# Block products for two gates: seven-product units, weight sums by accumulating transfers

## The chip, the cores and the metric

One core of a Trainium2 chip runs the whole kernel. The metric is the time of one execution on the device in microseconds (us); lower is better. Work is spread over five engines with instruction streams of their own: TensorE (PE) multiplies matrices, VectorE (DVE), ScalarE (ACT) and GpSimd (POOL) work on elements, SyncE (SP) issues transfers. DMA queues move data between DRAM and the on-chip memory. An engine executes its stream in order, and an instruction waits at the head of its stream until what it needs has been signalled.

## The reference

One step of a hybrid diffusion transformer on 128 context tokens and 512 latent tokens, 640 in all, with D = 1024. What bears on the change:

```python
def retention_branch(rq, rk, rv, rg, pos, dec_f, dec_b, s0_f, s0_b):
    ...
    o = rms_scale(o_f + o_b[:, :, ::-1])
    o = o.transpose(0, 2, 1, 3).reshape(B, L, RET_V)
    return jax.nn.silu(rg.astype(jnp.float32)) * o, s_f, s_b

def token_mixer(h, w_in, ...):
    z = h @ w_in
    q, k, v, rq, rk, rv, rg, ga, gr = jnp.split(z, np.cumsum(IN_SPLITS)[:-1].tolist(), axis=-1)
    ...
    ya = attend_blocks(q, k_all, v_all)
    yr, s_f, s_b = retention_branch(rq, rk, rv, rg, ret_pos, dec_f, dec_b, s0_f, s0_b)
    y = jax.nn.sigmoid(ga) * (ya @ w_att_o) + jax.nn.sigmoid(gr) * (yr.astype(h.dtype) @ w_ret_o)
    return y @ w_out, (k, v, s_f, s_b)
```

`rg` (1024 columns of w_in) is the output gate inside the retention branch, `gr` (1024 columns) the gate of the whole branch. After the mixer come a normalisation and a gated feed-forward part with a depthwise convolution (FFN).

## The kernel before

The tokens are five tiles of 128. Each matrix product is made of three: every operand is split into a high part (rounded to fp32r by ACT) and a low part (the rest, by DVE), and high x high, high x low and low x high are summed in PSUM. Weights come into `raw` buffers by SP's queue (two buffers of up to 1 MB, `w_raw`), their parts into `wh` buffers. ACT can also make a low part with DVE left out: it writes the negated weights, and a transfer issued by POOL adds the weights to it while it writes (an accumulating DMA; L150, L1148).

The stages around the change, in the order in which PE does them:

- States and retention (`states`, `retention`, until 498 us), with the first half of rg's columns (`rg0`) between its steps. `conv_load` (L1005) loads the constants of the FFN's convolution by four DMAs of SP, at step 1 of the retention (three of L1008, one of L1009). The reloads of the retention's queries, `qd` (L955), are in the same queue behind them.
- The second half of rg's columns by `a_group` (L175): five tiles of 128 tokens, the weights' 512 columns moving, 8 blocks of the inner dimension, 3 products: 120 matmuls of 512 columns. `evac_rg` (L1035) makes silu out of tanh and multiplies it onto `rvv`, the retention's normalised output.
- gr's columns by `gr_col` and `b_col` (L191): eight blocks of 128 columns as stationary operand, two halves of 320 tokens moving, 8 x 3 matmuls each: 384 of 320 columns. ACT writes the tanh of each half to `thr` (L1105). Between the first of them PE transposes `rvv` to yr (`yr_blocks`, L1067; ten blocks, each with four transpositions into one PSUM bank, and a split into a high and a low part). `ret_sums` builds the sums of quarters of yr on DVE (L1085 to L1097).
- `ret_unit` (four, from 586 us): yr @ w_ret_o for two blocks of 128 columns each. A unit is a two by two block product done with seven products of half sized blocks in place of eight; each product is four blocks of the inner dimension x 3 = 12 matmuls of 320 columns. The weight blocks B00, B01, B10, B11 are summed on DVE (`wsum`, L1131), the activations' quarters beforehand (`ret_sums`).

The seven products are numbered 1 to 7. 1, 6, 7 and 4 share one PSUM bank and pile up in it: ACT copies the bank out after 1 (L1181), after 6 (negated, L1185), after 7 (L1189) and after 4 (L1193), each before the next product is added into the bank. 2 has a bank of its own, 5 and 3 share a third. From the m=5 sum on, the buffer of B00 serves 5 (B00 + B01), then 6 (with B11 added), then 4 (with B10 added). `ret_pump` (L1219) queues the weights' preparation some products ahead, and `seq` is the order of the products in which product 4 of a unit is held back until two products of the next unit have been issued. PE, DVE and ACT keep the order of the code in these last two stages (`manual_schedule`); a scheduler orders the others and what is ahead.

## Time and profile before

| | |
|---|---|
| median of three runs | 1137.73 us (1137.13 to 1139.15) |
| profiled execution, time | 1138.44 us |
| its span, first to last instruction | 1136.7 us |
| its granted clock of TensorE | 0.998 of full speed |
| busy: PE, DVE, ACT, POOL | 1109.3, 844.2, 594.5, 142.9 us |
| retention ends, second half of rg | 498.5 to 525.8 us |
| gr with the transposition of yr | 525.8 to about 586 us |

A row of the timeline has start, length, engine, line, operation, output<-inputs, shape, and in brackets how long the engine had been idle and what ended that. A matmul's length includes its way through the array, so the rate of a row of them is read from the distance of their starts. A wait row names what waited, what it waited for, the total, how often, and the longest. "Landing" of a DMA is the time from its issue to its end.

### The profile page before, as it was taken

What the parts mean: (1) busy time and instruction counts of PE and PEld (TensorE: products, weight loads), DVE (VectorE), ACT (ScalarE), POOL (GpSimd) and SP (SyncE); (2) the same over time, 40 slices, a digit from 0 to 9 for tenths busy, and PEclk for the clock granted to TensorE, in tenths of its full rate; (3) what the DMA queues carried; (4) which work ended last, traced back from release to release, by engine and by line L of the source; (5) the groups of instructions that cost most, each with busy time, mean ns of one, the idle gap of its engine ahead of it and who ended that gap; (6) DMA issues with size and microseconds to landing.
All of it is one profiled execution on the core that took longest, in us unless ns stands there. A gap on an engine that the chain in (4) does not pass through costs nothing.

```text
span 1136.7 us, 17580 instructions
## 1 busy us (share of the span) xinstructions
PE 1109.3 (98%) x6757; PEld 1009.6 (89%) x6757; DVE 844.2 (74%) x1456; ACT 594.5 (52%) x1120; POOL 142.9 (13%) x171
## 2 busy tenths in 40 slices
...
GB/s 307 246 152 74 39 37 38 2 37 215 323 146 174 243 115 110 78 38 38 74 72 163 302 132 212 130 112 121 143 139 158 157 80 167 130 128 155 136 130 93
DMA packets 139316, 151.99 MB, mean 134 GB/s; under 512 B 27976, under 2 KB 108952, under 8 KB 138976
## 3 DMA queue, kind: packets, MB, share of 16 engines
...
q10 hardware_dynamic: 272, 0.11, 0.0%
...
## 4 chain that ended last, share of the span: by engine, by line
PE 88%; DVE 5%; ACT 3%; issue 2%; DMA 1%; SPq 0%; ACTq 0%; DVEq 0%; POOL 0%
DMA weights.raw.247_7726<-in_w_down 1%; DVE x1.u1.1_6330 L1496 1%; DMA ret2.qd.12_4681<-ret.u5.5_3422 0%; DMA const.u2.2_72<-in_b_mod 0%; DVE x1.u1.1_6330 L1545 0%; DVE x1.u1.1_6330 L1303 0%; PE mm3.mm.75_6171 L1176 0%; DVE acts.u2.2_91 L432 0%; PE mm1.mm.11_294 L161 0%; PE mm7.mm.59_10668 L1619 0%; PE mm7.mm.17_8071 L1619 0%; PE mm7.mm.41_9543 L1619 0%; PE mm7.mm.59_10668 L1618 0%; PE mm7.mm.44_9776 L1618 0%; PE mm7.mm.38_9294 L1619 0%
## 5 line engine op out<-in xcount | busy, mean ns | idle before, releaser
L1148 POOL DMA_DIRECT2D weights.wh.164_5865<-weights.raw.156_5798 x1 | 1.3, 1327 | 146.9 <-DVE f1.s.15_5209 L1187 146.9
L816 POOL DMA_DIRECT2D spill.u2.2_2891<-f1.s.1_1160 x1 | 0.6, 580 | 129.7 <-DVE mod.u3.3_2846 L604 129.7
L1633 DVE TENSOR_TENSOR t7.u4.4_6818<-t7.u4.4_6818,const.u1.1_70 128x320 f32<-128x320 f32 x10 | 4.9, 494 | 11.4 <-ACT const.u1.1_70 L1632 11.4
L152 DVE TENSOR_TENSOR weights.wh.113_4453<-weights.raw.111_4450,weights.wh.112_4452 128x1024 fp32r<-128x1024 f32 x1 | 1.2, 1227 | 13.1 <-ACT weights.wh.112_4452 L147 13.1
L938 DVE SCALAR_TENSOR_TENSOR ret2.u1.1_4263<-ret2.u1.1_4263,const.u11.11_86 64x128 f32<-64x128 f32 x24 | 6.8, 338 | 2.9 <-ACT ret2.u1.1_4263 L931 2.8
L940 DVE SCALAR_TENSOR_TENSOR ret2.u1.1_4263<-ret2.u1.1_4263,const.u11.11_86 64x128 f32<-64x128 f32 x24 | 6.6, 382 | 2.8 <-ACT ret2.u1.1_4263 L933 2.8
L429 ACT CAST acts.u1.1_90<-f0.s.2_104 128x640 fp32r<-128x640 f32 x4 | 2.9, 728 | 9.5 <-DVE f0.s.2_104 L427 9.5
L553 ACT ACTIVATE f0.s.3_710<-f0.s.3_710,p1q.ny20.11_878 128x128 f32<-128x128 f32 x20 | 6.0, 388 | 2.5 <-DVE p1q.ny20.11_878 L220 2.5
L446 PE MATMUL aux1.aux.1_134<-const.u1.1_70,const.u2.2_72 80*128 80x80 f32 x1 | 0.4, 367 | 7.1 <-DMA const.u2.2_72<-in_b_mod 7.1
L429 ACT CAST acts.u1.1_90<-f0.s.1_103 128x640 fp32r<-128x640 f32 x4 | 2.9, 727 | 8.3 <-DVE f0.s.1_103 L427 8.3
L299 POOL DMA_DIRECT2D mod.acc.24_3630<-in_b_mod x2 | 1.7, 858 | 42.5 <-ACT ret.u5.5_3422 L874 42.5
L147 ACT CAST weights.wh.67_3284<-weights.raw.66_3282 128x1024 fp32r<-128x1024 f32 x1 | 1.1, 1052 | 11.3 <-PE mm3.mm.8_3125 L198 11.3
L147 ACT CAST weights.wh.77_3520<-weights.raw.76_3518 128x1024 fp32r<-128x1024 f32 x1 | 1.0, 1048 | 11.2 <-PE mm3.mm.16_3382 L198 11.2
L584 POOL TENSOR_TENSOR p1.u1.1_604<-p1.u3.3_608,p1q.u1.1_598 128x512 f32<-128x512 f32 x1 | 1.3, 1302 | 44.5 <-DMA p1.u4.4_610<-in_cache_k 44.5
L1150 DVE TENSOR_TENSOR weights.wh.152_5717<-weights.raw.151_5663,weights.wh.152_5717 128x512 fp32r<-128x512 f32 x1 | 0.7, 693 | 8.3 <-ACT weights.wh.152_5717 L1141 8.3
L147 ACT CAST weights.wh.132_5219<-weights.raw.131_5217 128x1024 fp32r<-128x1024 f32 x1 | 1.1, 1055 | 11.0 <-PE mm3.mm.49_5037 L160 11.0
L1507 DVE TENSOR_TENSOR x1.u1.1_6330<-x1.u1.1_6330,gate.u1.1_6316 128x512 f32<-128x512 f32 x10 | 6.7, 693 | 0.0
L553 ACT ACTIVATE p1.u4.4_610<-p1.u4.4_610,p1.ny10.15_660 128x128 f32<-128x128 f32 x10 | 3.0, 389 | 6.5 <-DVE p1.ny10.15_660 L220 6.5
L1540 POOL TENSOR_TENSOR x1.u1.1_6330<-x1.u1.1_6330,weights.raw.422_10889 128x512 f32<-128x512 f32 x3 | 4.9, 1632 | 12.2 <-ACT x1.tm.111_10902 L1513 9.4
L446 PEld LDWEIGHTS aux1.aux.1_134<-const.u1.1_70,const.u2.2_72 80*128 80x128 f32 x1 | 0.2, 182 | 7.0 <-issue 7.0
L152 DVE TENSOR_TENSOR weights.wh.83_3656<-weights.raw.81_3653,weights.wh.82_3655 128x1024 fp32r<-128x1024 f32 x1 | 1.2, 1226 | 6.9 <-ACT weights.wh.82_3655 L147 6.9
L553 ACT ACTIVATE f0.s.4_959<-f0.s.4_959,p1q.ny20.20_1127 128x128 f32<-128x128 f32 x20 | 6.2, 396 | 0.0
...
## 6 DMA issues: line engine op xcount, KB each, us to landing
...
p0.u7.7_128<-in_w_mod SPq DMA_DIRECT2D x2, 1024.0 KB, 12.3
...
out_y_sample<-x1.u1.1_6330 SPq DMA_DIRECT2D x8, 256.0 KB, 2.2
```

Source lines behind the costliest of these rows:

```text
L147: nc.scalar.copy(hi, rv)
L152: (lo_eng or V).tensor_sub(lo, rv, hi.bitcast(F32))
L299: nc.gpsimd.dma_start(accs[v][0:1, c, :], a["b_mod"][0:1, col:col + DM], accum_op=ALU.add)
L429: nc.scalar.copy(hT[0][:, k, :], xk)
L553: nc.scalar.activation(x[:, j], x[:, j], AF.Copy, scale=rstd[:, j:j + 1])
L584: nc.gpsimd.tensor_mul(ct, r2[:, :, 0, :], gqk[:, i:i + 1, :].to_broadcast([P, 4, P]))
L938: V.scalar_tensor_tensor(Ss[0:64, hh, st + 1, j], Ss[0:64, hh, st, j], cdsel[0:64, h:h + 1], Ss[0:64, hh, st + 1, j], op0=ALU.mult, op1=AL ...
L940: V.scalar_tensor_tensor(Ss[64:128, hh, 2 - st, j], Ss[64:128, hh, 3 - st, j], cdsel[64:128, h:h + 1], Ss[64:128, hh, 2 - st, j], op0=ALU. ...
L1496: V.tensor_add(x1[:, t, gs], x1[:, t, gs], down_mul(ps, t, c0))
L1507: V.tensor_mul(x1[:, t, gs], x1[:, t, gs], gb[:, t == 0, gs])
L1540: eng.tensor_mul(x, x, fg[:, c0:c0 + 512])
L1633: V.tensor_sub(his[1], his[1], u3[i])
```

## The change

rg's second half and all of gr are computed by six units like the `ret_unit`s: `in_unit` (L1152), two for rg's four blocks of columns and four for gr's eight, each with seven products of 12 matmuls of 320 columns, in the order 1, 5, 2, 6, 3, 7, 4. The common part of both kinds of unit is `seven`, the activations' sums are built by `h_sums` during states and retention, partly by accumulating transfers of 655 KB. In an `in_unit` DVE makes only B00 + B01; the other three sums come from w_in in DRAM by accumulating transfers of 256 KB (L1179 and L1180 after the low part of m=5, L1182 after that of m=6). The low parts of m=2, and in four of the six units of m=3, come by an accumulating transfer too (L1173).

rg's second half is now there in transposed form, in `thr`; silu is applied there (`rg_col`), and the transposed second half of yr is multiplied with it (`yr_block`). yr's ten blocks are transposed one at a time between products (`when`), and so are the pieces of yr's sums; `y_diff` has one of its three operations done by an accumulating transfer (655 KB). Product 4 of the first six units is held back for 2, 2, 4, 4, 4, 2 products.

In `retention`, `conv_load` is called for one row at a time, at steps 2, 4, 6 and 8. `rg0`'s low parts come by accumulating transfers ("dma"). Some buffers move: the constants' row buffer, one of the rope tables, a sixth `r2k` buffer less, the `f1` buffers closed before the states.

```diff
-    def conv_load(after):
-        nc.gpsimd.tensor_copy(cw[:, :, 0], after)
-        for i in range(3):
-            nc.sync.dma_start(cw[:, i, :], a["conv_w"][0, i].rearrange("(c p) -> p c", p=P))
-        nc.sync.dma_start(cw[:, 3, :], a["conv_b"][0].rearrange("(c p) -> p c", p=P))
+    def conv_load(i, after):
+        nc.gpsimd.tensor_copy(cw[:, i, :1], after)
+        src = a["conv_w"][0, i] if i < 3 else a["conv_b"][0]
+        nc.sync.dma_start(cw[:, i, :], src.rearrange("(c p) -> p c", p=P))
...
-            if i == 1:
-                conv_load(sa[0][2][:, :4])
+            if i in (2, 4, 6, 8):
+                conv_load(i // 2 - 1, sa[i - 1][2][:, :1])
...
-    rg0 = a_group(w_in[:, O_RG:O_RG + 512], hTk, mm, evac_rg(0))
+    rg0 = a_group(w_in[:, O_RG:O_RG + 512], hTk, mm, evac_rg(0), "dma")
...
-    run(a_group(w_in[:, O_RG + 512:O_RG + 1024], hTk, mm, evac_rg(1)))
...
+        def diff(d, a, b):
+            for k in ks:
+                V.tensor_sub(d[:, k], a[0][:, k], b[0][:, k])
+                yield
+            nc.gpsimd.dma_start(d, a[1], accum_op=ALU.add)
+            yield
+            yield
+            for k in ks:
+                V.tensor_sub(d[:, k], d[:, k], b[1][:, k])
+                yield
...
+    def in_unit(c0, t0, col, lo_dma):
...
+        def prep(m):
+            if m == 5:
+                low_part()
+                V.tensor_add(bs[0, 0], bs[0, 0], bs[0, 1])
+            src = bs[SRC[m]]
+            hi, lo = halves_of(m, ops, src)
+            low_part()
+            if m in lo_dma:
+                nc.scalar.activation(lo, src, AF.Copy, scale=-1.0)
+                nc.gpsimd.dma_start(lo, src, accum_op=ALU.add)
+                return
+
+            def low():
+                V.tensor_sub(lo, src, hi.bitcast(F32))
+                if m == 5:
+                    nc.gpsimd.dma_start(bs[0, 0], quad(1, 1), accum_op=ALU.add)
+                    nc.gpsimd.dma_start(bs[0, 1], quad(1, 1), accum_op=ALU.add)
+                elif m == 6:
+                    nc.gpsimd.dma_start(bs[0, 0], quad(1, 0), accum_op=ALU.add)
+            lows.append(low)
...
+    units = [in_unit(O_RG + 512 + 2 * p * P, 4 + 2 * p, rg_col(4 + 2 * p), (2, 3)) for p in range(2)]
+    units += [in_unit(O_GR + 2 * p * P, 2 * p, gr_col(2 * p), (2, 3) if p % 2 else (2,)) for p in range(4)]
...
-    order = (1, 5, 6, 2, 3, 7, 4)
+    order = [(1, 5, 2, 6, 3, 7, 4)] * NU + [(1, 5, 6, 2, 3, 7, 4)] * NR
+    wait = [2, 2, 4, 4, 4, 2] + [2] * NR
...
-            for _ in gr_col(c, wg):
...
+        def yr_block(g, t):
+            pt = aux([P, 512], tag="aux")
+            for j in range(4):
+                nc.tensor.transpose(pt[:, j * P:(j + 1) * P], rvv[g][:, j, t, :], ident)
...
+            if g:
+                d = thr[:, 4:8, ts]
+                V.tensor_mul(d, d, p3)
+                p3 = d
+            split(yrT[0][:, 4 * g:4 * g + 4, ts], yrT[1][:, 4 * g:4 * g + 4, ts], p3)
+
+        def y_diff(a, b):
+            return [lambda: (V.tensor_sub(yx, yq[a][0], yq[b][0]), nc.gpsimd.dma_start(yx, yq[a][1], accum_op=ALU.add)),
+                    None, None, lambda: V.tensor_sub(yx, yx, yq[b][1])]
```

The order of the instructions shows three places. First ACT at gr's first blocks in the kernel before: tanh of a half straight from its bank (L1105), the casts of yr's blocks (L665) and of the weights (L147), the cast of a sum of yr (L1096).

```order
L1105 ACTIVATE rt.u1.1_5208<-mm3.mm.51_5299 128x320
L665 CAST yr.u1.1_5203<-aux3.aux.56_5346 128x4x128
L147 CAST weights.wh.137_5353<-weights.raw.136_5229 128x1024
L147 CAST weights.wh.139_5357<-weights.raw.136_5229 128x1024
L1105 ACTIVATE rt.u1.1_5208<-mm3.mm.52_5361 128x320
L1105 ACTIVATE rt.u1.1_5208<-mm3.mm.53_5387 128x320
L1096 CAST rt.u2.2_5415<-rt.u1.1_5208 128x1280
```

No cast there reads a buffer into which a transfer adds. Now ACT in the change, at the passage from unit 1 (banks mm.48, 49, 50) to unit 2 (weights raw.131; mm.51 is its first bank): wh.138 is m=4 of unit 1, wh.140 to 143 are m=1, 5, 2, 6 of unit 2; L1194 is the tanh of rg, L1128 and L1130 are the evictions of m=5 and m=6, L1138 that of m=4.

```order
L1148 CAST weights.wh.138_5253<-weights.raw.127_5126 128x512
L1126 COPY rt.u1.1_5107<-mm3.mm.48_5258 128x320
L1148 CAST weights.wh.140_5272<-weights.raw.131_5158 128x512
L1194 ACTIVATE aux3.aux.50_5275<-rt.u1.1_5107 128x320
L1194 ACTIVATE aux3.aux.51_5278<-rt.u1.1_5107 128x320
L1128 ACTIVATE rt.u1.1_5107<-mm3.mm.49_5281 128x320
...
L1148 CAST weights.wh.143_5346<-weights.raw.131_5158 128x512
L1194 ACTIVATE aux3.aux.54_5350<-rt.u1.1_5107 128x320
L1194 ACTIVATE aux3.aux.55_5353<-rt.u1.1_5107 128x320
L1130 ACTIVATE rt.u1.1_5107<-mm3.mm.48_5258 128x320
```

The eviction of unit 1's m=6 (last row) stands behind the cast of unit 2's m=6, which reads raw.131 after L1179's transfer.

POOL in the kernel before, from the retention to the first `ret_unit`s: the state outputs, the copy of `conv_load`, then the low parts and the additions of the attention branch.

```order
L927 DMA out_new_state_ret_fwd<-ret.r2k.26_4441 64x4x128
L928 DMA out_new_state_ret_bwd<-ret.r2k.26_4441 64x4x128
L1006 COPY const.u14.14_89<-ret2.rkT.6_4573 128x4
L1148 DMA weights.wh.164_5865<-weights.raw.156_5798 128x4x128
L1148 DMA weights.wh.165_5869<-weights.raw.156_5798 128x4x128
```

POOL in the change, units 2 and 3 (raw.131 and raw.139) with the first y_diff's transfer (L1357) among them:

```order
L1180 DMA weights.raw.131_5158<-in_w_in 128x4x128
L1179 DMA weights.raw.131_5158<-in_w_in 128x4x128
L1173 DMA weights.wh.142_5321<-weights.raw.131_5158 128x4x128
L1182 DMA weights.raw.131_5158<-in_w_in 128x4x128
L1357 DMA hs.b.5_4268<-yr.u2.2_5103 128x4x320
L1180 DMA weights.raw.139_5255<-in_w_in 128x4x128
L1179 DMA weights.raw.139_5255<-in_w_in 128x4x128
```

Between the constants' copies and the first `ret_unit` POOL now issues four or five transfers for each unit, L1180 ahead of L1179, and y_diff's in between.

DVE in the change at the same passage: unit 3's m=1 and 5 are wh.148 and 149, L1167 is the sum B00 + B01, L1195 the second operation of rg's gate, L1357 and L1358 the subtractions of y_diff, L1177 low parts.

```order
L1357 TENSOR_TENSOR hs.b.5_4268<-yr.u1.1_5102 128x1280
...
L1358 TENSOR_TENSOR hs.b.5_4268<-hs.b.5_4268,yr.u2.2_5103 128x1280
L1177 TENSOR_TENSOR weights.wh.148_5424<-weights.raw.139_5255,weights.wh.148_5424 128x512
L1195 SCALAR_TENSOR_TENSOR rt.u1.1_5107<-aux3.aux.56_5427,rt.u1.1_5107 128x320
L1195 SCALAR_TENSOR_TENSOR rt.u1.1_5107<-aux3.aux.57_5430,rt.u1.1_5107 128x320
L1167 TENSOR_TENSOR weights.raw.139_5255<-weights.raw.139_5255 128x4x128
```

L1358 stands ahead of unit 3's weight sum. In the kernel before, DVE had there the sums of yr in three operations each and no transfer between them:

```order
L1091 TENSOR_TENSOR rt.u1.1_5208<-rt.u1.1_5208,yr.u2.2_5204 128x1280
L1097 TENSOR_TENSOR yr.u2.2_5204<-rt.u1.1_5208,yr.u1.1_5203 128x4x320
L152 TENSOR_TENSOR weights.wh.148_5604<-weights.raw.146_5545,weights.wh.147_5603 128x1024
L152 TENSOR_TENSOR weights.wh.150_5608<-weights.raw.146_5545,weights.wh.149_5607 128x1024
L1150 TENSOR_TENSOR weights.wh.152_5717<-weights.raw.151_5663,weights.wh.152_5717 128x512
```

The transfer between L1357 and L1358 takes the place of an operation of DVE.

316 lines of the change are left out of this document (192 added, 124 removed).

## The prediction

> **What bounds the kernel now.** I read the page's shares first, with the share line of its chain.
>
> ```profile
> span 1136.7 us, 17580 instructions
> PE 1109.3 (98%) x6757; PEld 1009.6 (89%) x6757; DVE 844.2 (74%) x1456; ACT 594.5 (52%) x1120; POOL 142.9 (13%) x171
> PE 88%; DVE 5%; ACT 3%; issue 2%; DMA 1%; SPq 0%; ACTq 0%; DVEq 0%; POOL 0%
> ```
>
> TensorE (PE) works for 1109.3 of 1136.7 us. Then the view by stretches, over the retention (460 to 500), the gates (500 to 570) and the first blocks of the retention's projection (610 to 640); columns are the stretch, its length, busy us of PE, of PE's weight loads, of VectorE, ScalarE and GpSimd (DVE, ACT, POOL), granted clock, DMA share, GB/s. Below it, all waits of PE from 410 to 640.
>
> ```profile
> 420.00:460.00 40.00, 39.98 (x232) 34.57 (x232) 28.72 (x77) 20.34 (x37) 2.79 (x5) 1.00 0.56 107
> 460.00:500.00 40.00, 38.71 (x275) 35.32 (x274) 27.88 (x54) 21.42 (x45) 0.00 (x0) 1.00 0.42 67
> 540.00:570.00 30.00, 30.00 (x206) 30.00 (x206) 24.28 (x19) 11.74 (x16) 0.00 (x0) 1.00 0.22 70
> 610.00:640.00 30.00, 30.00 (x197) 29.18 (x197) 20.80 (x31) 15.59 (x31) 8.88 (x9) 1.00 1.01 222
> ```
> ```profile
> PE aux3.aux.33_4802 L980 <- DVE ret.r2k.39_4752 L982: 1.3, 1, 1.3
> PE mm3.mm.69_5909 L1176 <- ACT f1.s.18_5212 L1185: 0.2, 1, 0.2
> ```
>
> PE is the bound in all of it, at the full clock, and waits 1.5 us in 230. So columns that PE no longer multiplies come off the end one for one, and a wait that the change gives PE is added one for one. Both occur here.
>
> **The change, part by part.** First the columns. The starts of four matmuls, and of two transposed blocks of the retention's output (L1067, "T" below):
>
> ```profile
> 501.33 0.39 PE L159 MATMUL mm3.mm.46_5034<-weights.wh.122_5040,acts.u1.1_90 128*128 128x512 f32 x1
> 504.05 0.39 PE L159 MATMUL mm3.mm.47_5035<-weights.wh.122_5040,acts.u1.1_90 128*128 128x512 f32 x1
> 528.00 0.60 PE L1067 MATMUL aux3.aux.48_5251<-const.u1.1_70,f0.s.5_3419 128*128 128x128 f32 x4
> 528.44 0.60 PE L1067 MATMUL aux3.aux.49_5258<-const.u1.1_70,f0.s.5_3419 128*128 128x128 f32 x4
> 540.70 0.31 PE L197 MATMUL mm3.mm.53_5387<-acts.u1.1_90,weights.wh.132_5219 128*128 128x320 f32 x1
> 544.22 0.31 PE L197 MATMUL mm3.mm.54_5424<-acts.u1.1_90,weights.wh.137_5353 128*128 128x320 f32 x1
> ```
>
> Twelve matmuls of 512 columns lie between the first two (2.72 us, 0.227 each), 24 of 320 between the last two (3.52, 0.147 each). The old stage has 120 of the first and 384 of the second; the new one has 6 units x 7 products x 12 = 504 of the second. Gain: 120 x 0.080 = 9.6 us. A product costs 12 x 0.147 = 1.76 us, a T 0.44; the T's only change places.
>
> Now what feeds the products. Within an in_unit the weight sums that two products need (m=6: B00+B01+B11, m=4: that plus B10) are made by transfers that add w_in's blocks into the buffer (L1179, L1182), each issued after the low part of the product before it (m=5, then m=6). ACT, in order, casts m=6 only when the first has landed and m=4 only when the second has; what stands behind that cast on ACT waits with it. In the change's order the eviction of m=6 of unit 1 (L1130 from bank mm.48) stands behind the cast of m=6 of unit 2, and PE can't begin product (1,7), which writes the same bank, before that eviction; the same again one unit later.
>
> The prices: landings of today's accumulating transfers, one by one (256 KB rows L1148, a 320 KB one L1157), then min/median/max of the 256 KB ones of the FFN (L1599), of those of 512 KB (L150) and of those of 4 KB that add from DRAM (L299).
>
> ```profile
> f1.s.16_5210<-spill.u2.2_2891 POOLq DMA_DIRECT2D x1, 320.0 KB, 6.5
> weights.wh.164_5865<-weights.raw.156_5798 POOLq DMA_DIRECT2D x1, 256.0 KB, 4.3
> weights.wh.165_5869<-weights.raw.156_5798 POOLq DMA_DIRECT2D x1, 256.0 KB, 5.4
> weights.wh.173_5997<-weights.raw.160_5823 POOLq DMA_DIRECT2D x1, 256.0 KB, 7.2
> weights.wh.180_6111<-weights.raw.168_5906 POOLq DMA_DIRECT2D x1, 256.0 KB, 8.3
> ```
> ```profile
> DMA to landing us min/median/max: 4.1/4.3/5.7
> ```
> ```profile
> DMA to landing us min/median/max: 4.5/4.8/8.7
> ```
> ```profile
> DMA to landing us min/median/max: 2.2/2.7/2.9
> ```
>
> L1182 flies mostly alone: 4.3. L1179 is issued right behind L1180 of the same size, as wh.165 is behind wh.164: 5.4. The bounds are 4.1 and 8.3. (The Trainium skill, "DMA: Bandwidth & Descriptors", section "Anatomy of one DMA — SWDGE (gpsimd) path", gives about 2.0 us plus the bytes at 436 GB/s, so an estimate of 2.6 us for 256 KB; the rows above, 4.3 to 8.3 for that size, disagree, and by its figure the sum would come out as the first rival below.)
>
> The steps between, on ACT and DVE:
>
> ```profile
> 540.90 0.44 ACT L1105 ACTIVATE rt.u1.1_5208<-mm3.mm.52_5361 128x320 f32<-128x320 f32 x1 [1.03 <-PE mm3.mm.52_5361 L199]
> 553.28 1.26 ACT L1096 CAST f0.s.7_5413<-rt.u1.1_5208 128x1280 fp32r<-128x1280 f32 x1 [1.38 <-DVE rt.u1.1_5208 L1087]
> 601.38 0.62 ACT L1141 CAST weights.wh.167_5904<-weights.raw.156_5798 128x512 fp32r<-128x512 f32 x1 [1.50 <-DVE weights.raw.156_5798 L1131]
> 601.90 0.42 ACT L1181 COPY f1.s.17_5211<-mm3.mm.69_5909 128x320 f32<-128x320 f32 x1
> 600.20 0.48 DVE L1190 TENSOR_TENSOR f1.s.16_5210<-f1.s.16_5210,f1.s.15_5209 128x320 f32<-128x320 f32 x1
> 600.60 0.69 DVE L1131 TENSOR_TENSOR weights.raw.156_5798<-weights.raw.156_5798 128x512 f32<-128x512 f32 x1
> 602.03 0.69 DVE L1150 TENSOR_TENSOR weights.wh.167_5904<-weights.raw.156_5798,weights.wh.167_5904 128x512 fp32r<-128x512 f32 x1 [0.74 <-ACT weights.wh.167_5904 L1141]
> L1097 DVE TENSOR_TENSOR f0.s.7_5413<-rt.u1.1_5208,f0.s.7_5413 128x1280 fp32r<-128x1280 f32 x1 | 1.5, 1492 | 1.3 <-ACT f0.s.7_5413 L1096 1.3
> ```
>
> Cast 0.62 (0.52 until ACT's next start, as 601.38 and 601.90 show), eviction 0.42, tanh of a half 0.44, DVE's weight sum or low part 0.69, a half's addition 0.48; of 1280 columns the cast 1.26, DVE's operation 1.49.
>
> *Place A*, from the end of product (0,5) to the start of (1,7). ACT: eviction of (0,5) and the cast of a T (0.9), casts of m=4 of unit 0 and m=1 of unit 1 (1.0); DVE: low part, an addition, sum for m=5 (1.9); cast and low part of m=5 (1.3): 5.2 in all. L1179: 5.4. Cast and low part of m=6: 1.3. L1182: 4.3. Cast of m=4 0.6; eviction of (1,1), cast of m=1 of unit 2, two tanh 1.8; second gate operation, split of a T, weight sum on DVE 1.9; cast and low part of m=5 of unit 2 1.3; L1179: 5.4; cast 0.6, two tanh 0.9, eviction of m=6 of unit 1 0.4. Sum 29.1. PE has in that time ten products and five T's: 17.6 + 2.2 = 19.8. It stands still for 9.3.
>
> *Place B*, from (1,7) to (2,7): 7 products and two T's, 13.2. The cast of m=6 of unit 2 ended 1.3 before (1,7) began; after it two tanh, two gate operations on DVE and the first subtraction of y_diff (L1357, 1.49) end 1.6 after that start. Then y_diff's transfer adds 655 KB: 512 KB take 4.8, scaled by bytes 6.0 (bounds 5.6 and 10.9). DVE's next operation in y_diff waits for it, and behind it on DVE stands unit 3's weight sum. So 1.6 + 6.0 + 1.5 (y_diff) + 0.7 + 1.0 + 0.7 (low part, two gate operations, sum) = 11.5, cast and low part 1.3, L1179 5.4, then 1.9 as at the end of A: 20.1. Stall 6.9.
>
> *Place C*, from (2,7) to (4,7): 14 products and three T's, 26.0. The evictions of m=6 now stand ahead of the casts of m=6, so fewer chains add up. The second y_diff begins its subtraction 8.8 after the start, behind the addition of (3,2), and ends 10.3; its transfer flies beside unit 4's three, so I take 8.0 between its bounds: 18.3; L1358 1.5; the cast and low part of m=4, which wait for L1182, on POOL behind that transfer, 3.6; DVE's low part of y_diff's result (L1369) 1.5; low part and sum for m=5 1.4; cast of m=5, cast and copy of m=2 1.8; eviction 0.4: 28.5. Stall 2.5. Afterwards unit 5 has four products, 7.0, before (5,6), and its L1179 with cast and low part is done after 5.8: none.
>
> Together 18.7. At 4.1 for every 256 KB landing, 5.6 for y_diff and casts at 0.52, A is 6, B 5 and C nothing: 11. At 8.3 and 10.9 A is 19, B 15, C some 8: 42.
>
> *The retention.* PE's wait of 1.3 comes with these rows of SP's queue: the constants of the convolution (L1008, L1009) stand ahead of the reloads of qd (L955).
>
> ```profile
> 451.46 7.78 SPq L1008 DMA_DIRECT2D const.u14.14_89<-in_conv_w  x3
> 459.28 3.32 SPq L1009 DMA_DIRECT2D const.u14.14_89<-in_conv_b  x1
> 466.51 2.56 SPq L955 DMA_DIRECT2D ret2.qd.12_4681<-ret.u5.5_3422  x4
> ```
>
> One row at a time delays such a reload by at most 3.3 instead of 11.1, so the 1.3 should go. Against it, DVE gets the activation sums (20 pieces of half of 1280 columns, about 0.8 each: 16) and unit 0's preparations (2.8), and loses rg0's four low parts (4.9): 14 more in 80 us of which 56.6 were busy (28.72 + 27.88). They fit; but one piece ahead of an operation for which PE waits costs up to 0.8, at ten groups of heads and tiles up to 8. I take 0, bounds -1.3 and +8. rg0's low parts by transfers, h3's and h4's low parts at the stage's start and the constants' and buffers' new places lie ahead of their use by several products: 0.
>
> **The sum.** 1138.4 (the profiled run; its span is 1136.7) - 9.6 + 18.7 + 0 = 1147.5. That run lies 0.7 above the median of the three, 1137.7, so 1147 on the median's scale, which all times below have too.
>
> **Rivals.** *The sums land early enough* (faster). If a quarter-megabyte accumulation took what L299's small ones take, 2.7, and y_diff's 4.8 at the most, A would fall by 7.0 (2 x 2.7 + 1.6) to 2.3, B by 3.9 (2.7 + 1.2) to 3.0, C to nothing: 1137.7 - 9.6 + 5.3 = 1133, and 1128 with no stall. For it: these transfers meet nearly idle DMA engines (share 0.22 at 540 to 570, against 1.01 at 610 to 640, where the 5.4 to 8.3 were taken). Against it: no transfer of that size landed in under 4.1, the FFN's included. By the Trainium skill's figure of 2.6 on that page, an estimate, this case would come about.
>
> *A draw*: landings at their minima, 11 of stalls against 9.6 and the 1.3 that goes in the retention: 1138.
>
> *VectorE and the queues are crowded in the retention* (slower): from 1.5 pieces of DVE in each of ten groups on, PE waits there for 5 to 8 as well: 1152 to 1155, and to 1158 if the reloads of qd wait on DMA engines beside h_sums' two transfers of 655 KB.
>
> *The engines of the transfers become the bound* (slower): each unit moves a load of 1 MB and 4 or 5 accumulations of 256 KB. If all landings go as the later ones at 610 to 640 (7 to 8.3), A is 15 to 19, B 11 to 15, C 5 to 8: stalls of 31 to 42, 1159 to 1170.
>
> *It doesn't do what it says*: the products count 504, whichever way they are fed, so the 9.6 are there; what can fail is only that they reach the end.
>
> **How the numbers follow.** Forecast (1141 to 1152) 0.52; first rival (1128 to 1135) 0.19; draw 0.10; crowded retention 0.10; engines full 0.09. ±0.2% of 1137.7, some 2.3 us, is about what a measurement of this kernel can tell: 1135.4 to 1140.0 is the draw with the forecast's lower edge, 0.11. Faster 0.19, slower 0.70. The range leaves out the fuller half of the last case and the better part of the first: 1131 to 1163; the forecast's own is 1141 to 1152.
>
> **What would show it.** In the changed profile: 320-column matmuls at 0.147 through the whole stage (else the 9.6 are wrong); waits of PE at the seventh product of units 1 and 2 and 4 for ACT's eviction of m=6, of about 9, 7 and 2; on ACT ahead of them idle time ended by a DMA into weights.raw; on DVE idle time before L1358. L1179's landings of 5 or more, L1182's of 4 or more. No wait for ret.r2k in the retention over 1. It would be wrong if PE's waits in the stage summed to under 7, if landings came under 3.5, or if over 5 us of new waits lay ahead of the stage.

## The result: 1182.77 us, 45 slower

| | before | changed |
|---|---|---|
| median us (lowest to highest) | 1137.43 (1136.84 to 1139.15, 4 runs) | 1182.77 (1180.83 to 1183.28, 4 runs) |
| ratio, 95% interval | | 1.0393 [1.0375, 1.0411] |
| span of the profiled run, us | 1136.7 | 1180.8 |
| waits of PE from 395 to 660 us, summed | 1.5 | 38.8 |

The forecast was 1147 (1131 to 1163), slower with 0.70. The sign holds, the size doesn't, and the time lies outside the range. The page of the changed kernel, first its share lines, then its chain's:

```profile
span 1180.8 us, 17844 instructions
PE 1115.7 (94%) x6757; PEld 1016.7 (86%) x6757; DVE 871.3 (74%) x1519; ACT 628.7 (53%) x1193; POOL 190.2 (16%) x210
PE 78%; DVE 8%; DMA 4%; ACT 4%; issue 3%; SPq 2%; POOL 1%; ACTq 0%; DVEq 0%; POOLq 0%
```

PE now has work for 94% of the span, where it was 98%, and transfers (DMA 4%, SP's queue 2%) stand on the chain. PE's busy time rose by 6.4 although 9.6 us of columns are gone, so the matmuls that are left take 16.0 longer. That is the first sign of the term that the forecast lacks, the clock. Three of the stretches shown of before, in the same columns:

```profile
420.00:460.00 40.00, 35.14 (x185) 29.98 (x184) 25.53 (x65) 20.96 (x35) 8.75 (x12) 0.91 0.79 171
460.00:500.00 40.00, 32.41 (x221) 28.66 (x221) 27.28 (x60) 19.52 (x43) 5.92 (x7) 1.00 0.79 86
...
540.00:570.00 30.00, 19.71 (x118) 18.92 (x117) 16.22 (x25) 13.10 (x28) 10.34 (x8) 0.89 0.81 147
```

PE has lost its full rows, the clock is under 1 in two of them, and the share of the DMA engines in the last rose from 0.22 to 0.81. DVE is less busy than before in all three; it waits as well. The stage is what follows the retention: the six in_units, with (1,7) for product 7 of unit 1. The longest of 13 waits of PE in the states, the retention and the stage; the six left out come to 5.6:

```profile
PE mm3.mm.48_5258 L1121 <- ACT rt.u1.1_5107 L1130: 6.2, 1, 6.2
PE aux3.aux.61_5535 L1347 <- DVE rt.u1.1_5107 L1195: 5.7, 1, 5.7
PE mm3.mm.57_5719 L1121 <- ACT rt.u1.1_5107 L1126: 5.4, 1, 5.4
PE aux3.aux.13_4486 L971 <- DVE ret.r2k.26_4483 L968: 4.8, 1, 4.8
PE mm3.mm.45_5112 L1121 <- ACT rt.u1.1_5107 L1130: 4.1, 1, 4.1
PE mm3.mm.60_5848 L1121 <- ACT rt.u1.1_5107 L1126: 3.6, 1, 3.6
PE aux3.aux.33_4832 L1031 <- DVE ret.r2k.38_4778 L1033: 3.4, 1, 3.4
```

The rows of mm and of L1347 belong to the stage (26.4 with the small ones), those of aux.13 and aux.33 to states and retention (12.4 with the small ones). The stage's first product begins here; the row of the kernel before is the first product of rg's second half there:

```profile
512.79 0.39 PE L1121 MATMUL mm3.mm.45_5112<-acts.u1.1_90,weights.wh.123_5076 128*128 128x320 f32 x1
```
```profile
498.48 0.48 PE L159 MATMUL mm3.mm.45_5033<-weights.wh.122_5040,acts.u1.1_90 128*128 128x512 f32 x1
```

So 14.3 of the 44.1 us between the spans are lost ahead of the stage and 29.8 behind its start. Ahead of it the waits account for 11.1 (12.4 less the 1.3 of before). In the stage -9.6 of columns and 26.4 of waits make 16.8. The rest, 3.2 and 13.0, together 16.2, is no wait. The view by stretches over the wait of aux.13 shows what most of it is (the last three columns are granted clock, DMA share and GB/s):

```profile
440.00:445.00 5.00, 0.65 (x3) 0.19 (x1) 4.96 (x16) 3.66 (x4) 0.12 (x1) 0.89 0.38 146
445.00:450.00 5.00, 4.52 (x15) 3.97 (x16) 5.00 (x15) 3.14 (x5) 3.03 (x4) 0.50 0.77 140
450.00:455.00 5.00, 5.00 (x30) 4.39 (x29) 2.16 (x7) 2.19 (x4) 1.31 (x1) 0.93 1.05 193
```

Behind the wait PE works at half its clock for about 5 us. Matmuls of 512 columns there and then:

```profile
448.60 0.63 PE L159 MATMUL mm3.mm.41_4455<-weights.wh.112_4461,acts.u1.1_90 128*128 128x512 f32 x1
449.03 0.63 PE L160 MATMUL mm3.mm.41_4455<-weights.wh.113_4462,acts.u1.1_90 128*128 128x512 f32 x1
...
450.96 0.40 PE L159 MATMUL mm3.mm.41_4455<-weights.wh.114_4466,acts.u1.1_90 128*128 128x512 f32 x1
451.19 0.39 PE L160 MATMUL mm3.mm.41_4455<-weights.wh.115_4467,acts.u1.1_90 128*128 128x512 f32 x1
```

They start 0.43 apart, then 0.23. Cut into stretches of 5 us, the window from 395 to 660 has 13 with a clock under 0.99; their missing clock adds up to 18.7 us, an upper bound since part of it falls into the waits themselves. Weighted with PE's busy time in the same stretches it is 13.8, so the clock is some 14 of the 16.2; the other 2 aren't traced. In the kernel before no stretch there is under 0.99.

How the sums hold the stage up, on ACT; L1148 is the cast of a weight block, L1130 the eviction of m=6:

```profile
532.13 0.62 ACT L1148 CAST weights.wh.135_5208<-weights.raw.127_5126 128x512 fp32r<-128x512 f32 x1 [4.54 <-DMA weights.raw.127_5126<-in_w_in]
...
549.79 0.62 ACT L1148 CAST weights.wh.143_5346<-weights.raw.131_5158 128x512 fp32r<-128x512 f32 x1 [4.37 <-DMA weights.raw.131_5158<-in_w_in]
...
551.05 0.41 ACT L1130 ACTIVATE rt.u1.1_5107<-mm3.mm.48_5258 128x320 f32<-128x320 f32 x1
```

Both casts wait more than 4 us for an accumulating transfer into their buffer, five others wait 3.1 to 5.1, and the eviction for which mm.48 waits 6.2 stands behind the second. The landings of L1179, then of L1182:

```profile
DMA to landing us min/median/max: 5.1/5.3/6.2
```
```profile
DMA to landing us min/median/max: 4.6/4.8/5.7
```

The wait of 4.1 at (0,7), bank mm.45, is not for a landing. Its eviction stands on ACT, at 526.70, behind the cast of unit 1's m=5, and that waits for DVE's sum:

```profile
524.41 0.68 DVE L1167 TENSOR_TENSOR weights.raw.127_5126<-weights.raw.127_5126 128x512 f32<-128x512 f32 x1
```
```profile
525.13 0.62 ACT L1148 CAST weights.wh.133_5179<-weights.raw.127_5126 128x512 fp32r<-128x512 f32 x1 [3.12 <-DVE weights.raw.127_5126 L1167]
```

DVE is at the retention's last products (L1054) until 520.3, then at h3's low part (L1338, 1.48), four more low parts and an addition; so it reaches the sum at 524.4.

Later on DVE, y_diff's second subtraction waits for y_diff's transfer, 2.62 the first time and 2.30 the second:

```profile
560.08 1.49 DVE L1358 TENSOR_TENSOR hs.b.5_4268<-hs.b.5_4268,yr.u2.2_5103 128x1280 f32<-128x1280 f32 x1 [2.62 <-DMA hs.b.5_4268<-yr.u2.2_5103]
```

Ahead of the stage, on DVE, an addition of `h_sums` (L934) waits for the sum's transfer, and a product of the states (L1020) for the reload of qd.4; a piece of the sums (L948) stands directly ahead of the r2k.26 that aux.13 waits for. Below it what that reload took to land (2.3 before):

```profile
414.48 1.56 DVE L934 TENSOR_TENSOR weights.raw.116_4492<-weights.raw.116_4492,acts.u2.2_91 128x640 f32<-128x640 f32 x2 [7.67 <-DMA weights.raw.116_4492<-acts.u2.2_91]
...
431.94 0.69 DVE L1020 TENSOR_TENSOR ret2.qd.4_4573<-ret2.qd.4_4573,ret.u2.2_3418 128x512 f32<-128x512 f32 x1 [4.34 <-DMA ret2.qd.4_4573<-ret.u4.4_3422]
...
443.84 0.82 DVE L948 TENSOR_TENSOR hs.b.4_4267<-weights.raw.116_4492,hs.b.3_4266 128x640 fp32r<-128x640 f32 x1
444.58 0.75 DVE L968 TENSOR_TENSOR ret.r2k.26_4483<-ret.u3.3_3421,const.u11.11_87 128x256 f32<-128x256 f32 x2
```
```profile
ret2.qd.4_4573<-ret.u4.4_3422 SPq DMA_DIRECT2D x4, 64.0 KB, 7.9
```

Unit 0's weight sums come during the retention, and there too a cast waits for L1179:

```profile
476.40 0.62 ACT L1148 CAST weights.wh.126_5089<-weights.raw.122_4985 128x512 fp32r<-128x512 f32 x1 [3.39 <-DMA weights.raw.122_4985<-in_w_in]
```

DVE, which has that block's low part next, stands still for 4.2 and then for 4.4 more until another reload (qd.12) is there; r2k.38, for which aux.33 waits 3.4, comes behind both.

### The profile page after: what moved, and what is told of

The parts are those of the page before. It is cut to its first block, busy times and chain, and to the rows that moved or that the text cites. A ratio compares the mean times of both kernels' runs of the same rounds, so it can differ in the third digit from the quotient of the medians.

```text
span 1180.8 us, 17844 instructions
## 1 busy us (share of the span) xinstructions
PE 1115.7 (94%) x6757; PEld 1016.7 (86%) x6757; DVE 871.3 (74%) x1519; ACT 628.7 (53%) x1193; POOL 190.2 (16%) x210
## 4 chain that ended last, share of the span: by engine, by line
PE 78%; DVE 8%; DMA 4%; ACT 4%; issue 3%; SPq 2%; POOL 1%; ACTq 0%; DVEq 0%; POOLq 0%
SPq L1006 1%; DMA hs.b.5_4268<-yr.u2.2_5103 1%; DMA weights.raw.155_5570<-in_w_in 1%; DMA hs.b.5_4268<-acts.u2.2_91 1%; DMA weights.raw.127_5126<-in_w_in 1%; DMA weights.raw.266_7926<-in_w_down 1%; DVE ret2.u1.1_4272 L990 1%; DVE x1.u1.1_6530 L1630 1%; DMA weights.raw.131_5158<-in_w_in 0%; DMA xin.u1.1_72<-in_b_mod 0%; ACT yr.u1.1_5102 L665 0%; DVE x1.u1.1_6530 L1679 0%; DMA ret2.qd.12_4701<-ret.u4.4_3422 0%; DVE rt.u1.1_5107 L1352 0%; DVE yr.u2.2_5103 L666 0%
## 5 line engine op out<-in xcount | busy, mean ns | idle before, releaser
L988 DVE SCALAR_TENSOR_TENSOR ret2.u1.1_4272<-ret2.u1.1_4272,const.u10.10_86 64x128 f32<-64x128 f32 x24 | 6.8, 338 | 2.8 <-ACT ret2.u1.1_4272 L981 2.8
L553 ACT ACTIVATE f0.s.3_710<-f0.s.3_710,p1q.ny20.11_878 128x128 f32<-128x128 f32 x20 | 6.0, 388 | 2.5 <-DVE p1q.ny20.11_878 L220 2.5
L934 DVE TENSOR_TENSOR weights.raw.116_4492<-weights.raw.116_4492,acts.u2.2_91 128x640 f32<-128x640 f32 x2 | 1.6, 822 | 7.7 <-DMA weights.raw.116_4492<-acts.u2.2_91 7.7
L147 ACT CAST weights.wh.67_3284<-weights.raw.66_3282 128x1024 fp32r<-128x1024 f32 x1 | 1.1, 1052 | 11.3 <-PE mm3.mm.8_3125 L198 11.3
L147 ACT CAST weights.wh.77_3520<-weights.raw.76_3518 128x1024 fp32r<-128x1024 f32 x1 | 1.1, 1050 | 11.2 <-PE mm3.mm.16_3382 L198 11.2
L990 DVE SCALAR_TENSOR_TENSOR ret2.u1.1_4272<-ret2.u1.1_4272,const.u10.10_86 64x128 f32<-64x128 f32 x24 | 6.6, 380 | 0.1
L1358 DVE TENSOR_TENSOR hs.b.5_4268<-hs.b.5_4268,yr.u2.2_5103 128x1280 f32<-128x1280 f32 x2 | 3.0, 1494 | 4.9 <-DMA hs.b.5_4268<-yr.u2.2_5103 4.9
L1347 PE MATMUL aux3.aux.61_5535<-const.u1.1_70,f0.s.6_3420 128*128 128x128 f32 x4 | 1.1, 428 | 5.7 <-DVE rt.u1.1_5107 L1195 5.7
```

Source lines behind the costliest of these rows:

```text
L553: nc.scalar.activation(x[:, j], x[:, j], AF.Copy, scale=rstd[:, j:j + 1])
L988: V.scalar_tensor_tensor(Ss[0:64, hh, st + 1, j], Ss[0:64, hh, st, j], cdsel[0:64, h:h + 1], Ss[0:64, hh, st + 1, j], op0=ALU.mult, op1=AL ...
L990: V.scalar_tensor_tensor(Ss[64:128, hh, 2 - st, j], Ss[64:128, hh, 3 - st, j], cdsel[64:128, h:h + 1], Ss[64:128, hh, 2 - st, j], op0=ALU. ...
L1358: None, None, lambda: V.tensor_sub(yx, yx, yq[b][1])]
```

## The experiments

Each kernel's ratio is taken against runs of the kernel before on the same chip, with medians of 1137.43 to 1138.43 there. "Waits" are PE's from 395 to 660 us in the profiled run.

| kernel | median us | ratio, 95% interval | waits |
|---|---|---|---|
| changed | 1182.77 | 1.0393 [1.0375, 1.0411] | 38.8 |
| units' weight sums on VectorE | 1165.71 | 1.0237 [1.0217, 1.0257] | 27.9 |
| activations' sums on VectorE | 1180.52 | 1.0367 [1.0349, 1.0385] | 35.3 |
| both, and y_diff on VectorE ("all sums on VectorE") | 1159.32 | 1.0177 [1.0155, 1.0199] | 24.6 |
| the last, rg0's low parts on VectorE | 1156.66 | 1.0170 [1.0153, 1.0187] | 19.5 |
| all sums on VectorE, activations' sums left out | 1153.76 | 1.0145 [1.0129, 1.0160] | 19.6 |
| all sums on VectorE, late preparation | 1157.17 | 1.0175 [1.0160, 1.0190] | 20.7 |
| before, constants by rows | 1137.59 | 0.9998 [0.9989, 1.0008] | 1.0 |
| gr alone, sums on VectorE | 1152.52 | 1.0128 [1.0112, 1.0143] | 16.0 |
| gr alone, weight sums by transfers | 1161.58 | 1.0205 [1.0186, 1.0223] | 21.1 |
| no activations' and no units' weight sums | 1134.01 | 0.9953 [0.9935, 0.9971] | 4.3 |
| the same, rg0's low parts on VectorE | 1127.68 | 0.9905 [0.9890, 0.9919] | 1.2 |
| rg0's low parts on VectorE, weight sums on GpSimd | 1154.17 | 1.0144 [1.0129, 1.0159] | 16.6 |
| the same, late preparation | 1152.74 | 1.0128 [1.0108, 1.0147] | 16.7 |
| gr alone, weight sums on GpSimd | 1147.48 | 1.0087 [1.0070, 1.0104] | 10.0 |

**The weight sums.** VectorE makes the three sums that came by transfers.

```diff
-            if m == 5:
-                low_part()
-                V.tensor_add(bs[0, 0], bs[0, 0], bs[0, 1])
+            if m in (5, 6):
+                low_part()
+            if m in (4, 5, 6):
+                add = {5: (0, 1), 6: (1, 1), 4: (1, 0)}[m]
+                V.tensor_add(bs[0, 0], bs[0, 0], bs[add])
...
+            if m == 5:
+                V.tensor_add(bs[0, 1], bs[0, 1], bs[1, 1])
```

> The changed kernel, with the 18 accumulating transfers of the weight sums (L1179, L1180, L1182) replaced by three additions on DVE a unit, as in the four units after them; all else, the order of the instructions on ACT and PE too, is kept. Theory A (ACT's in-order casts wait for these landings, evictions behind them hold PE, and each wait of over 3.5 us is followed by some 5 us at half the granted clock): the four long waits at products (1,7), T of the second half, (4,6) and (5,6), 21 us together, go to under 3, the half-clock stretches behind them (about 9 us) with them; the time falls from 1182.8 to 1150-1158. What is left is the retention's loss (14) and the wait at (0,7). Theory B (DVE is as short of time there as the transfers: it gets 18 x 0.69 = 12.4 us more): the waits move to DVE, the time falls by under 12, to 1170 or more.

1165.71: 17.1 less, between the two expectations. The wait at (1,7), bank mm.48, falls from 6.2 to 1.0, those at (5,6) and at aux.33 in the retention are gone, and the stage begins 3.5 earlier, at 509.28; but four others stay:

```profile
PE mm3.mm.45_5111 L1121 <- ACT rt.u1.1_5106 L1130: 5.5, 1, 5.5
PE aux3.aux.13_4486 L971 <- DVE ret.r2k.26_4483 L968: 4.9, 1, 4.9
PE mm3.mm.57_5719 L1121 <- ACT rt.u1.1_5106 L1126: 4.8, 1, 4.8
PE aux3.aux.61_5534 L1344 <- DVE rt.u1.1_5106 L1192: 3.9, 1, 3.9
```

The landings of the weight sums cost 17 us; they aren't the whole cause.

**The activations' sums.**

```diff
-            nc.gpsimd.dma_start(d, a[1], accum_op=ALU.add)
-            yield
-            yield
+            for k in ks:
+                V.tensor_add(d[:, k], d[:, k], a[1][:, k])
+                yield
```

> The changed kernel, with the two accumulating transfers of the activation sums (L930, 655 KB each, during states and retention) replaced by four additions of half of 1280 columns on DVE. Theory A (DVE, in order, stands still for 7.7 us before L934 for the first transfer and never catches up, so PE waits 4.8 for it in the states and runs at half the clock behind it): that wait and its half-clock stretch go, 7 to 8 us; the later waits of 3.4 and 1.5 stay: 1174-1177. Theory B (the transfers also hold the reloads of qd, so the whole 14 us of the retention hang on them): 1166-1170. Theory C (the 15 us of added DVE work are the cause, whoever adds): no change or slower, 1181-1185.

1180.52, 2.3 less with overlapping intervals: the transfers that L934 waits for are hardly the cause of the loss in states and retention.

**All sums on VectorE.** The first two edits, and in `y_diff`:

```diff
-            return [lambda: (V.tensor_sub(yx, yq[a][0], yq[b][0]), nc.gpsimd.dma_start(yx, yq[a][1], accum_op=ALU.add)),
-                    None, None, lambda: V.tensor_sub(yx, yx, yq[b][1])]
+            return [lambda: V.tensor_sub(yx, yq[a][0], yq[b][0]), lambda: V.tensor_add(yx, yx, yq[a][1]),
+                    None, lambda: V.tensor_sub(yx, yx, yq[b][1])]
```

> The changed kernel with every sum on DVE: both edits above, and y_diff's third operation (L1357) on DVE too. The only accumulating transfers left are the low parts (L1173, L150). Theory A: the waits of the stage go, the two long DVE waits before L1358 (4.9) too, and the retention's first wait: 1141-1150. If DVE is the next bound (Theory B): 1160 or more.

1159.32: of the 45 us, 23 go with these transfers and some 22 don't. Waits of 24.6 are left, the longest (5.5) at (0,7) again, and the casts of the units still wait, now for the additions (1.36 at unit 1's m=6, where it was 4.54).

**The clock by itself.** The kernel before, with a growing chain of copies on ACT ahead of a transposition at seven places of gr, so that PE waits; nothing else changes. One profiled run.

```diff
+            if c < KD - 1:
+                nc.scalar.copy(probe, thr[:, c, :512])
+                for _ in range((1, 3, 4, 5, 6, 8, 12)[c]):
+                    nc.scalar.copy(probe, probe)
+                pp = aux([P, 512], tag="aux")
+                nc.tensor.transpose(pp[:, :P], probe[:, :P], ident)
```

> The kernel before, with PE made to wait on purpose after seven of the eight blocks of gr: ACT makes a chain of 2, 4, 5, 6, 7, 9 and 13 copies of 128x512 behind the block's last tanh, and PE has to transpose the result before it goes on; the waits should be about 1.5 to 7.5 us in rising order, some 14 us or more apart. Theory A (a wait of over about 3.5 us is followed by half the granted clock for some 5 us, a shorter one by nothing): the waits up to 3 cost themselves, those from 4 on themselves and 2 to 3 us more, and the clock in the stretch behind them shows 0.5. Theory B (the half clock of the changed kernel has to do with its transfers): the clock stays at 1.0 and the time rises by the sum of the waits alone.

The time is 1186.25, 48.5 more. The seven waits sum to 33.6, so some 15 aren't these waits. The two shortest, and the stretches behind them:

```profile
541.16 0.33 PE L1250 MATMUL aux3.aux.57_5356<-const.u1.1_70,rt.u2.2_5209 128*128 128x128 f32 x1 [1.84 <-ACT rt.u2.2_5209 L1248]
551.65 0.47 PE L1250 MATMUL aux3.aux.58_5422<-const.u1.1_70,rt.u2.2_5209 128*128 128x128 f32 x1 [3.12 <-ACT rt.u2.2_5209 L1248]
```
```profile
540.00:545.00 5.00, 3.84 (x27) 3.84 (x28) 3.58 (x4) 2.98 (x4) 0.00 (x0) 1.00 0.02 3
...
550.00:555.00 5.00, 3.35 (x15) 3.35 (x16) 2.11 (x2) 2.69 (x4) 0.00 (x0) 0.66 0.00 0
```

After the wait of 1.84 the clock stays, after that of 3.12 and each longer one it halves. In stretches of 0.1 us the half clock lasts 3.5, 6.9 or 10.4 us, and for 3 to 5.5 of that PE is working again. Of the 15 us some 2.5 belong to the retention: aux.33 waits 2.1 here (1.3 in the kernel before), and a half clock of 3.5 follows that, too. The other 12.4, which hold the seven transpositions, are 2.1 for each of six waits; PE's busy time in the stretches of 0.1 us times the missing clock gives 1.9. In the changed kernel the same product is 14.4 for its six half-clock stretches, 2.4 each. The Trainium skill, "TensorE: Matmul & The Clock Gate", section "Part 1: The HAM clock gate (the "warmup" mystery)", has a gate that watches the array's activity in a free-running window of about 3.4 us and passes half the clock until the array has been busy that long. These rows agree, with lengths that are multiples of about 3.5. The bound isn't sharp: 2.1 sufficed here, and in the changed kernel the clock stayed at 1.00 after the wait of 3.4.

**rg0's low parts on VectorE**, otherwise all sums on VectorE.

```diff
-    rg0 = a_group(w_in[:, O_RG:O_RG + 512], hTk, mm, evac_rg(0), "dma")
+    rg0 = a_group(w_in[:, O_RG:O_RG + 512], hTk, mm, evac_rg(0))
```

> The kernel with all sums on DVE (e3_all_dve, 1159.3), with the low parts of rg's first half on DVE again, as in the kernel before, in place of accumulating transfers (L150, four of 512 KB). In e3 and in the changed kernel the first reload of the retention's queries (qd.4, 64 KB) landed after 7.7 and 7.9 us where it took 2.3 in the kernel before, DVE waited 4.4 for it, and PE 4.6 in the states later. Theory A (those 512 KB transfers hold the reload): qd.4 lands in 2 to 3 again, the wait of 4.6 and the half clock behind it go: 1152-1154. Theory B (DVE has more work there than fits; it gets 4.9 us more): the wait stays at 4 to 9: 1159-1165.

1156.66, 2.7 less at the median, but the intervals of the ratios overlap. The trace is clearer: the reload of qd.4 lands in 3.1, where with rg0's transfers it took 7.7, and the wait for aux.13 falls from 4.6 to 2.9. PE's waits fall by 5.1, but the half clock shows four times here and twice in the run it is compared with.

```profile
ret2.qd.4_4572<-ret.u4.4_3422 SPq DMA_DIRECT2D x4, 64.0 KB, 3.1
```

**No activations' sums.** All sums on VectorE, but the sums of the activations (hT), with their casts and low parts, aren't made, and quarters of hT stand in for them; this leaves out part of the computation.

```diff
-    hs = {1: [quarter("a", 2) for _ in range(2)], 2: [quarter("b", 3) for _ in range(2)], 4: hq[1, 0]}
+    hs = {1: hq[1, 1], 2: hq[0, 0], 3: hq[0, 1], 4: hq[1, 0]}
```

> The kernel with all sums on DVE (e3_all_dve, 1159.3) without the activations' sums at all: products 5, 6, 7 and 3 of the six units get quarters of h in their place, so 24 pieces of DVE work (about 19 us), 5 casts of 1280 columns on ACT and the buffers' waits are left out; PE's work is the same. Theory A (the added DVE and ACT work in states and retention is what holds PE there): the waits of 4.6 and 1.5 in states and retention go with their half clock, and (0,7) waits 1.5 to 3 less since L1338's 1.5 and the cast of 1.3 no longer stand ahead: 1146-1150. Theory B (the transfers there do it): the 4.6 stays, 1155-1159.

1153.76, 5.6 less. The retention's own waits (1.5 and less) go; aux.13 still waits 3.1, with qd.4 landing in 8.1, and (0,7) 5.0.

**Late preparation.** The next unit's preparation begins up to two products later.

```diff
-            ret_pump(n + 1, min(5 + n, 8))
+            ret_pump(n + 1, min(5 + max(n - 2, 0), 8))
```

> The kernel with all sums on DVE (e3_all_dve, 1159.3), with one number changed: the weights' preparation may run less far ahead in the stage's first five products, so that ACT's eviction of product 6 of unit 0 (L1130) stands ahead of the cast of unit 1's m=5 instead of behind it and two more. Theory A (product (0,7), 5.5 us of wait in e3, 4.1 in the changed kernel, waits for that eviction only because of what stands ahead of it on ACT): the wait falls to 0.5 to 2, its half-clock stretch goes, 1153-1156; a part may come back at unit 1, whose weights are prepared later. Theory B (everything is late there by the retention's end on DVE): it stays over 3.5 and the time within 2 of 1159.

1157.17, within the interval of the kernel without it. The wait at (0,7) falls from 5.5 to 2.0, that at (1,7) rises from 0.7 to 2.5: the lateness is passed on.

**Constants by rows**, in the kernel before: `conv_load` as in the change, nothing else.

> The kernel before (1137.7) with the change's fourth part alone: the convolution's constants loaded one row at a time, at steps 2, 4, 6 and 8 of the retention. The prediction's term: the wait of 1.3 for ret.r2k goes, 1136-1137. Rival: each row's transfer, of elements of 4 bytes, delays a reload by its own landing, and the wait comes back at other steps: 1137-1139.

1137.59 against 1137.58. The wait of 1.3 becomes two of 0.6 and 0.2; this part of the change is worth nothing that can be measured.

**gr alone.** Four units for gr with all sums on VectorE; rg's second half as before with the activations' sums made beside it, rg0's low parts on VectorE, the constants by rows. Product 4 is held back for two products in every unit, and yr's transpositions and sums are spread anew (these lines are left out here).

```diff
-    units = [in_unit(O_RG + 512 + 2 * p * P, 4 + 2 * p, rg_col(4 + 2 * p), (2, 3)) for p in range(2)]
-    units += [in_unit(O_GR + 2 * p * P, 2 * p, gr_col(2 * p), (2, 3) if p % 2 else (2,)) for p in range(4)]
+    units = [in_unit(O_GR + 2 * p * P, 2 * p, gr_col(2 * p), (2, 3) if p % 2 else (2,)) for p in range(4)]
...
+    run(rg0)
+    for i, _ in enumerate(a_group(w_in[:, O_RG + 512:O_RG + 1024], hTk, mm, evac_rg(1))):
+        for _ in range(4):
+            next(hsum, None)
```

> One part of the change alone: only the retention branch's gate (the four units of 512 inner rows) goes by seven products; the second half of the output gate is computed as in the kernel before, with its eight plain products, and so has neither its transposed tiles nor its larger units. All sums of weights, activations and tiles are made by VectorE. By rows of the trace the columns saved are 4 units x 12 products x (0.227 - 0.147) = about 3.9 us where each unit saves one product of eight, up to 48 x 0.147 = 7.0 us as the issue counts them. Theory A (the waits left in the kernel of all VectorE sums, 1159, come from the second half's part: its preparation that runs into the retention, its tanh tiles and the wait before its transposition): the waits go to under 5 us and the time comes to 1133 to 1143. Theory B (ScalarE's casts and VectorE's sums for any unit of seven products cost more than the products saved, at about 16 to 17 of each 20 us on VectorE): waits of 3 us and more stay before the four units, the clock halves behind them, and the time is 1145 or more.

1152.52: theory B. gr had products of 320 columns before, so the columns saved are the expectation's 7.0, not its 3.9. Without rg's transposed tiles and with more lead the units still make PE wait, 16.0 in all, each for ScalarE or VectorE.

**The same with transfers.** `low` issues L1179, L1180 and L1182 again.

> The kernel of the part alone (retention branch's gate by seven products, second half as before), with one thing put back: the weight sums of the four units are made by accumulating transfers instead of VectorE additions. Theory A (each unit's chain of two accumulating transfers of 4.1 to 6.2 us between ScalarE's casts makes PE wait, whatever stands ahead of it): waits of 3 to 6 us come back at one to three of the four units, with the clock at half behind each, and the time is 10 to 20 us over the kernel with the additions. Theory B (the transfers hurt only because the second half's units stand ahead of them and ScalarE is late already): within 4 us of the kernel with the additions.

1161.58, 9.1 more on the same chip: a little under what theory A said and well over B's 4. Two long waits come back, both for the eviction of m=6:

```profile
PE mm3.mm.53_5427 L1120 <- ACT rt.u1.1_5270 L1129: 6.1, 1, 6.1
PE mm3.mm.56_5582 L1120 <- ACT rt.u1.1_5270 L1129: 3.5, 1, 3.5
```

**No sums.** The kernel without activations' sums, its units' weight sums left out too, so the products take blocks as they are loaded; the edit is against that kernel.

```diff
-            if m in (4, 5, 6):
-                add = {5: (0, 1), 6: (1, 1), 4: (1, 0)}[m]
-                V.tensor_add(bs[0, 0], bs[0, 0], bs[add])
...
-            if m == 5:
-                V.tensor_add(bs[0, 1], bs[0, 1], bs[1, 1])
```

> The kernel without the activations' sums (1153.8 us), with the weight sums of its units of seven products left out as well: neither transfers nor additions make them, the units cast their blocks as they are loaded. Casts, low parts, products, the pieces of the retention and the sums of the output tiles stay. Theory A (after the transfers are gone the rest of the loss is VectorE's time for the sums: at about 16 to 17 of each 20 us ScalarE's casts wait 1.4 us each for them): the waits of PE in the stage go, the nearly 10 us of columns appear, and the time is 1128 to 1140. Theory B (the rest is the smaller unit itself: seven casts and seven low parts in an order that leaves the two engines too little room, and the preparation that runs into the retention): waits of 3 us and more stay at the first unit and at the row before the retention's states, and the time is 1146 or more.

1134.01: 19.7 less than with the sums, and under the kernel before. The seven casts and low parts of a unit fit; what doesn't is the sums between them. Two waits are left.

```profile
PE aux3.aux.13_4482 L940 <- DVE ret.r2k.26_4479 L937: 2.9, 1, 2.9
PE mm3.mm.45_5073 L1090 <- ACT rt.u1.1_5072 L1099: 1.4, 1, 1.4
```

**The same, rg0's low parts on VectorE** (the edit shown above).

> The same, with the low weight parts of the retention gate's first group made by VectorE instead of accumulating transfers. Theory A (those transfers delay the reload of the states' first tile to nearly 8 us and so the last wait of the retention): 3 to 5 us below the kernel with the transfers, the wait ahead of the states under 1.5 us, and the time is near or below that of the kernel before (1128 to 1138). Theory B (the wait there is VectorE's and ScalarE's own work ahead of the states, whatever the reload takes): within 1.5 us of the kernel with the transfers.

1127.68, another 6.3 less. The wait ahead of the states is gone, and the only one left is (0,7)'s, 1.2. qd.4 lands in 2.5 there, and no stretch has a clock under 0.99. The 10.75 under the kernel before are the 9.6 of columns and 0.3 less of waits; 0.9 is left over.

**The weight sums on GpSimd**, with rg0's low parts on VectorE: the four additions of a unit by `nc.gpsimd.tensor_add`.

> The kernel with all sums and the first group's low parts on VectorE (1156.7 us), with the four weight sums of each unit moved on to GpSimd's adder. GpSimd took 1.6 us for an addition of 128x512 in the block at the program's end, VectorE 0.69. VectorE is relieved of 24 x 0.69 = 16.4 us; in the chain from one product's operands to the next each sum then takes 0.9 more. Theory A (the loss of that kernel is VectorE's time: without these sums it ran at its full gain): the time comes to 1133 to 1145. Theory B (the loss is the length of each unit's chain of casts and sums, by whichever engine): waits stay at the same products or grow, and the time is 1154 or more.

1154.17, 2.5 less at the median, with overlapping intervals, at the edge of theory B. PE waits at the same products. The sum on GpSimd, made in place, waits for VectorE's low part of the product before (first row), and the cast for the sum:

```profile
519.10 1.26 POOL L1169 TENSOR_TENSOR weights.raw.127_5123<-weights.raw.127_5123 128x512 f32<-128x512 f32 x1 [5.77 <-DVE weights.wh.132_5158 L1180]
```
```profile
520.39 0.62 ACT L1148 CAST weights.wh.133_5177<-weights.raw.127_5123 128x512 fp32r<-128x512 f32 x1 [3.47 <-POOL weights.raw.127_5123 L1169]
```

VectorE is rid of 24 additions, 16.4 us, but its busy time over the span falls by only 7.4 (891.9 to 884.5). Other operations of it take longer beside an addition on GpSimd, as this low part, 0.68 to 0.70 in the kernel without:

```profile
565.57 1.68 POOL L1173 TENSOR_TENSOR weights.raw.147_5404<-weights.raw.147_5404 128x512 f32<-128x512 f32 x1
```
```profile
566.18 1.62 DVE L1180 TENSOR_TENSOR weights.wh.157_5620<-weights.raw.147_5404,weights.wh.157_5620 128x512 fp32r<-128x512 f32 x1
```

**With late preparation too.**

> The kernel with the weight sums on GpSimd, with the preparation of the next unit begun two products later in the first units, as in the earlier run where that took 2.2 us off. Theory A: 1 to 4 us off again, at the first unit. Theory B (the chain is longer on GpSimd, and a later start makes later units wait more): the same or up to 6 us slower.

1152.74: 1.4 less at the median, within the intervals. The wait at (0,7), 4.4, goes, and one of 3.3 comes at a transposition behind it.

**gr alone, sums on GpSimd.**

> The kernel with the retention branch's gate alone by seven products (1152.5 us), with the four weight sums of its four units on GpSimd's adder. Theory A (VectorE's time): 1132 to 1142, with waits of PE under 4 us in the stage. Theory B (the chain's length): 1150 or more.

1147.48, between the two: 5.0 less than with VectorE's sums, and still 0.9% over the kernel before. VectorE's busy time fell by 6.7 here for 16 additions, 11.0 us. No version with units that makes all its sums ran faster than the kernel before.

## Why the prediction was wrong

*The columns* were right. A product's matmuls start 0.146 to 0.147 apart wherever the clock is full, and with the sums left out and rg0's transfers gone the kernel runs 10.75 us under the one before.

*Place A* had its mechanism right: the eviction for which (1,7) waits stands behind the cast that waits for L1179, and the wait falls to 1.0 when VectorE makes the sums. From the end of (0,5) to the start of (1,7) the working has 29.1; it took 35.1 (516.4 to 551.5). Nearly all of the excess lies at the start of the chain: unit 1's first sum, L1167, was done 8.7 after (0,5), where the working has 3.8, and the rest took 26.4 for 25.3. That step failed: the working put h3's and h4's low parts at 0 and had nothing for the retention's last operations on VectorE. That lateness made a wait that was not in the working, 4.1 at (0,7), which stays at 5.0 to 5.5 with the sums on VectorE and falls to 1.4 without them. That both waits together, 10.3, are close to the 9.3 is in part luck.

*Place B*: 6.9 forecast, 5.7 measured, on the transposition just ahead of (2,7). It waits for the second gate operation (L1195), which stands behind the cast of unit 3's m=6; that begins at 570.55, 5.3 after L1179's transfer was issued, and L1179 comes behind y_diff as in the working. *Place C* came at (4,6) instead of (4,7), 5.4 for 2.5, and *unit 5*, forecast without one, waited 3.6 at (5,6). Both wait for the eviction after the first product (L1126), which stands behind a cast of m=4 and in unit 4 also behind the cast of y_diff's result; the working followed only the eviction of m=6. L1179's median of 5.3 was forecast as 5.4, L1182's 4.8 as 4.3; y_diff's 6.4 and 8.3 as 6.0 and 8.0. The prices of the landings held. What didn't is the chain's start and the order in later units. The stalls came to 26.4 where "Together 18.7" stood.

*The retention* was the first failed step: "I take 0, bounds -1.3 and +8" was +14.3. "They fit" compared sums of busy time over 80 us. Three things came in between. The sentence that let rg0's low parts by transfers count for nothing priced only what they take from VectorE; beside these transfers the reload of qd.4 took 7 to 8 us (2.5 and 3.1 without them, in two pairs of runs). The pieces of the activations' sums stand in DVE's order ahead of the r2k that PE waits for. Either of these alone leaves a wait of 2.8 to 3.1 at aux.13; with both gone it is gone. And unit 0's weight sums, whose 2.8 counted only VectorE's work, hold ACT and DVE for L1179's landing; without these transfers the wait of 3.4 at aux.33 goes. The start of the stage shows it step by step: 512.8 in the changed kernel, 509.3 with the weight sums on VectorE, 507.1 with all sums there, 504.0 with rg0's low parts there too, and 496.1 with no sums and rg0's low parts there; 498.5 in the kernel before. The reloads' path past the constants changed nothing: the rows, one by one, gave 1137.59.

*The missing term* is the clock, some 14 of the 16.2 us that are no waits: 3.2 of these lie ahead of the stage and 13.0 in it. "A wait that the change gives PE is added one for one" is false for the longer waits: the six from 3.6 up cost about 2.4 more each. The probe shows the same without any of the change's transfers, at about 2 each. Had the term been there, the forecast's own stalls of 9.3 and 6.9 would have brought only about 5.

So by terms: columns right, stalls 7.7 too low, retention 14.3 too low (3.2 of it no wait), and 13.0 of the stage that are no wait, mostly the clock, not foreseen; together 35, of which the forecast's distance is made.

*The rivals.* "The engines of the transfers become the bound" came nearest in time (1159 to 1170) by a mechanism that didn't occur in the stage: L1179 stayed at 5.1 to 6.2, far from 7 to 8.3. In the states something of its kind did occur, at the reloads. "VectorE and queues crowded in the retention" did occur, beside the forecast's case and not in its place; the two should have been added. The draw needed landings of 4.1, and L1179 took 5.1 at the least. "The sums land early enough" has its answer in the kernel with sums on VectorE: even additions of 0.69 in the landings' place leave waits of up to 5.5, though they also take VectorE's time.

*What stays open.* The units' weight sums cost 19.7 us when VectorE makes them in 16.4 of work. Moving them to GpSimd gained 2.5, which is not clear of the noise, and 5.0. That separates two causes only in part: it lengthens the chain low part, sum, cast, low part in one buffer (1.26 for a sum in place of 0.69), and it took less than half of the 16.4 off VectorE. So the length of that chain, in turns on two or three engines, is a likely cause beside VectorE's time, but it isn't shown, and how the 19.7 divide wasn't settled. Sums into buffers of their own, which would cut the chain, weren't tried.
